# Four transfers of 8 to 15 small packets, issued by ScalarE in the middle of a rotary-embedding kernel

## The chip, the cores and the metric

The kernel runs on one core of one Trainium2 chip. The metric is device time in microseconds (us) of one execution. The core's engines are TensorE (PE; PEld is its weight load), VectorE (DVE), ScalarE (ACT), GpSimd (POOL) and SyncE (SP); 16 transfer (DMA) engines move data between HBM and the on-chip memory. The kernel before ran on the same chip beside the others. Kernels are compared only within the same rounds.

## The reference

Rotary embedding over 16 sequences of 512 rows, 16 heads of 64 values: 32 MiB in, 32 MiB out.

```python
x = x.reshape(batch, seq, num_heads, head_dim)       # 16, 512, 16, 64, float32
x1, x2 = x[..., :half_dim], x[..., half_dim:]
rotated = np.concatenate([x1 * cos - x2 * sin, x1 * sin + x2 * cos], axis=-1)
```

## The kernel before

The work is cut into eight tiles of 4 MiB (128 partitions of 32 KiB, two sequences each). Five buffers hold tiles; a tile is rotated in place and stored from the same buffer. SyncE issues every transfer, in the order written: load 0 in two parts with the two tables between, loads 1 to 4, then stores as tiles become ready. Loads 5 to 7 need buffers whose stores (0 to 2) have landed, so they come behind store 2. The last store is cut in two.

```python
    def load(t, lo=0, hi=KK):
        ...
        nc.sync.dma_start(out=tiles[t][:, s], in_=x_v[t][:, s])

    def store(t, lo=0, hi=KK):
        s = slice(lo * dim, hi * dim)
        nc.sync.dma_start(out=out_v[t][:, s], in_=tiles[t][:, s])
    ...
    def finish(t):
        add(0)
        ...                                  # store(t), the last tile in two parts
        if t + 1 == NT - BUFS:               # behind store 2
            for n in range(BUFS, NT):
                load(n)

    for t in range(NT):                      # NT = 8 tiles
        xt = tiles[t]
        for k in range(KK):                  # 8 rows of 1024 values per partition
            ...   # GpSimd and VectorE multiply by sin, VectorE by cos,
            ...   # TensorE + ScalarE add the two (k = 0 and 4), VectorE adds the rest
            if k == 0 and t > 0:
                finish(t - 1)
            add(1)
    finish(NT - 1)
```

Each transfer raises a completion semaphore when it has landed. The program has eight of them and the tile framework hands them out in turn, to transfers of all issuing engines alike. A transfer that gets a semaphore again waits until the earlier user has landed: in the changed kernel store 3 is next on the semaphore of the first small transfer. The turn goes by the instruction order of the built program, which is not that of the source: the small transfers added below are written behind store 2 and loads 5 to 7, but the built program lists them before store 2.

Of the kernel before, what the change touches and what calls it, by code (L numbers as in the profile page):

```python
# [8 lines left out]
FP32 = mybir.dt.float32  # L9
# [12 lines left out]

FIRST = (3, 8)
LAST_OUT = (4, 8)


@with_exitstack
def kernel(
# [13 lines left out]
    nc = tc.nc  # L42
# [7 lines left out]
    NT = batch // NB  # L50
# [5 lines left out]
    sin_v = sin.rearrange("(p k) j -> p (k j)", k=KK)  # L56

    fixed = ctx.enter_context(tc.tile_pool(name="fixed", bufs=1))
# [10 lines left out]
    def load(t, lo=0, hi=KK):  # L69
        if tiles[t] is None:  # L70
            tiles[t] = xp.tile([P, F], FP32, name="xt")
# [6 lines that stand above are left out]
# [15 lines left out]
    for i in range(3):  # L93
        ps = pe.tile([P, BANK], FP32, name="ps")
        nc.tensor.matmul(out=ps, lhsT=zero[:, :P], rhs=zero, start=True, stop=True)  # L95

    sns = fixed.tile([P, KK, 2, half], FP32)
    tab = pfix.tile([P, BANK], FP32)
    cos_t = tab[:, : KK * half]
# [14 lines left out]
    def cos_b(k, n):  # L114
        c = cos_t[:, k * half : (k + 1) * half]
        return bass.AP(tensor=c.tensor, offset=c.offset, ap=[c.ap[0], [0, n], [1, half]])

    def over_heads(s):
        return bass.AP(tensor=s.tensor, offset=s.offset, ap=[s.ap[0], [0, nh], [1, hd]])

    def swapped(r, n):
        return bass.AP(
            tensor=r.tensor, offset=r.offset + half, ap=[r.ap[0], [hd, n], [-half, 2], [1, half]]
        )

    def swapped_signed(k):

        i = on_dve.index(k)
        s = sns_t[:, i * hd : (i + 1) * hd]
        return bass.AP(  # L130
            tensor=s.tensor, offset=s.offset + half, ap=[s.ap[0], [0, nh], [-half, 2], [1, half]]
        )

    def pairs(r):
        return r.rearrange("p (a j) -> p a j", j=half)

    def halves(r):
        return r.rearrange("p (h a j) -> p h a j", a=2, j=half)
# [3 lines left out]
    def add(most):  # L142
        while len(pending) > most:
            r, ps, b = pending.pop(0)
            nc.vector.tensor_tensor(out=r, in0=ps, in1=b, op=ALU.add)  # L145

    def finish(t):
        add(0)
        lo = 0
        for hi in LAST_OUT if t == NT - 1 else (KK,):  # L150
            store(t, lo, hi)
            lo = hi
        if t + 1 == NT - BUFS:
            for n in range(BUFS, NT):
                load(n)

    for t in range(NT):
        xt = tiles[t]
        for k in range(KK):
            r = xt[:, k * dim : (k + 1) * dim]  # L160
            own = k in DVE_B[t % 2]
            if not own:
                b = bp.tile([P, dim], FP32, name="b")
                sk = sns[:, k].rearrange("p a j -> p (a j)")
                nc.gpsimd.tensor_tensor(out=halves(b), in0=swapped(r, nh), in1=over_heads(sk), op=ALU.mult)  # L165
            if k in PE_ROWS[t % 2]:
                parts = []
                for c in range(0, dim, BANK):
                    ps = pe.tile([P, BANK], FP32, name="ps")
                    rc = r[:, c : c + BANK]  # L170
                    nc.vector.tensor_tensor(  # L171
                        out=pairs(ps), in0=pairs(rc), in1=cos_b(k, BANK // half), op=ALU.mult
                    )
                    parts.append((ps, rc, swapped(rc, BANK // hd) if own else b[:, c : c + BANK]))
                if own:
                    nc.vector.tensor_tensor(out=halves(r), in0=halves(r), in1=swapped_signed(k), op=ALU.mult)  # L176
                for ps, rc, rhs in parts:
                    nc.tensor.matmul(out=ps, lhsT=ident, rhs=rhs, start=False, stop=True, skip_group_check=True)  # L178
                    nc.scalar.copy(out=rc, in_=ps)  # L179
            else:  # L180
                add(1)
                ps = pd.tile([P, dim], FP32, name="pd")
                nc.vector.tensor_tensor(out=pairs(ps), in0=pairs(r), in1=cos_b(k, 2 * nh), op=ALU.mult)  # L183
                pending.append((r, ps, b))
            if k == 0 and t > 0:
                finish(t - 1)
            add(1)
    finish(NT - 1)


# [33 lines left out]
```

## Time and profile before

| | kernel before |
|---|---|
| time, first three runs | 162.77 us median (162.58 to 162.78) |
| span in the profile | 160.8 us |
| transfers | 20, moving 67.26 MB in 2754 packets |
| rate | 418 GB/s over the span, 434 GB/s between landings |
| transfer engines busy | 97.9% of the span |
| VectorE / GpSimd / ScalarE busy | 88% / 81% / 12% |

The prediction below shows the lines and how to read them.

### The profile page before, as it was taken

The page shows a single profiled execution, that of the slowest core. Times are in us where ns is not written, and L with a number is a line of the kernel's source. Part 1 is how long each engine was busy: PE and PEld are TensorE (multiplying, and loading weights), DVE is VectorE, ACT ScalarE, POOL GpSimd, SP SyncE. Part 2 cuts the span into 40 slices and gives each one's busy share as a digit, 9 for nine tenths or more (in the row PEclk, how much of TensorE's full clock was granted, in tenths as well). Part 3 has the DMA queues.
Part 4 walks back from the last instruction along what each step waited for, and adds up shares of the span by engine and source line. Part 5 has one row for each costly group of instructions (what it writes and reads, how often), then busy time and mean ns, then how long its engine had stood idle before and what let it go on. Part 6 is the DMA issues. An engine that isn't in the chain of part 4 may idle for free. (4 is left out here: it accounts for less than half of the span.)

```text
span 160.8 us, 524 instructions
## 1 busy us (share of the span) xinstructions
PE 62.3 (39%) x71; PEld 20.0 (12%) x71; DVE 141.4 (88%) x142; ACT 20.0 (12%) x33; POOL 130.3 (81%) x62
## 2 busy tenths in 40 slices
PE   3045380546217260708035440918053721735000
PEld 0022020202011110202020200211020201111000
DVE  1059999999999999999999999999999999999800
ACT  0110220021102020111102020112002110202000
POOL 1039999999999999999999899999999799950000
PEclk9999958576956755595555555555955585587655
DMA  5999999999999999999999999999999999999994
GB/s 186 395 423 463 408 481 416 391 497 416 391 489 416 402 416 481 408 391 505 399 399 481 424 399 475 424 408 432 465 399 432 465 408 432 457 416 408 428 428 179
DMA packets 2754, 67.26 MB, mean 418 GB/s; under 512 B 320, under 2 KB 448, under 8 KB 448
## 3 DMA queue, kind: packets, MB, share of 16 engines
q1 hardware_dynamic: 2752, 67.24, 97.9%
q14 instruction: 2, 0.02, 0.0%
HBM read 33.69 MB, written 33.55 MB: 418 GB/s over the span
## 5 line engine op out<-in xcount | busy, mean ns | idle before, releaser
L165 POOL TENSOR_TENSOR b<-xt,sns 128x1024 f32<-128x1024 f32 x56 | 129.6, 2358 | 11.8 <-DVE sns L108 9.4
L183 DVE TENSOR_TENSOR pd<-xt,tab 128x1024 f32<-128x1024 f32 x48 | 58.1, 1225 | 0.8
L145 DVE TENSOR_TENSOR xt<-pd,b 128x1024 f32<-128x1024 f32 x48 | 58.4, 1218 | 0.0
L178 PE MATMUL ps<-xt,ident 128*128 128x512 f32 x32 | 29.5, 1077 | 48.6 <-issue 38.1
L178 PE MATMUL ps<-b,ident 128*128 128x512 f32 x32 | 29.4, 1073 | 29.8 <-DVE ps L171 27.1
L179 ACT COPY xt<-ps 128x512 f32<-128x512 f32 x32 | 18.7, 585 | 120.3 <-PE ps L178 120.3
L171 DVE TENSOR_TENSOR ps<-xt,tab 128x512 f32<-128x512 f32 x32 | 20.6, 688 | 0.0
L178 PEld LDWEIGHTS ps<-xt,ident 128*128 128x128 f32 x32 | 9.4, 324 | 68.2 <-issue 63.6
L178 PEld LDWEIGHTS ps<-b,ident 128*128 128x128 f32 x32 | 9.2, 316 | 49.7 <-issue 25.6
L176 DVE TENSOR_TENSOR xt<-xt,tab 128x1024 f32<-128x1024 f32 x8 | 9.8, 1221 | 0.4
L107 DVE TENSOR_SCALAR sns<-tab 128x256 f32<-128x256 f32 x1 | 0.4, 424 | 8.2 <-PE tab L105 8.2
L104 PE MATMUL tab<-b,spread 64*128 64x256 f32 x2 | 1.2, 696 | 5.1 <-DMA b<-in_sin_dram 5.1
L179 ACT ACT_TABLE_LOAD x1 | 1.3, 1283 | 7.3 <-DMA xt<-in_x_dram 7.3
L95 PE MATMUL ps<-zero 128*128 128x512 bf16 x3 | 1.5, 626 | 1.2 <-DVE zero L92 1.2
L104 PEld LDWEIGHTS tab<-b,spread 64*128 64x128 f32 x2 | 0.5, 307 | 6.0 <-issue 6.0
L105 PE MATMUL tab<-b,spread 64*128 64x256 f32 x2 | 1.1, 631 | 0.0
L92 DVE MEMSET zero<- 128x256 uint32 x1 | 0.3, 272 | 0.9 <-PEq L205 0.9
L105 PEld LDWEIGHTS tab<-b,spread 64*128 64x128 f32 x2 | 0.7, 333 | 0.2
L103 DVE COPY spread<-ident 64x64 f32<-64x64 f32 x2 | 0.3, 184 | 0.2 <-POOL ident masks.py:199 0.2
L95 PEld LDWEIGHTS <-zero 128*128 128x128 bf16 x3 | 0.3, 124 | 1.5 <-DVE zero L92 1.2
masks.py:197 POOL MEMSET ident<- 128x128 f32 x1 | 0.2, 205 | 0.3 <-POOLq L205 0.3
L108 DVE COPY sns<-tab 128x256 f32<-128x256 f32 x1 | 0.4, 414 | 0.0
(6 smaller groups left out, 0.9 us busy)
## 6 DMA issues: line engine op xcount, KB each, us to landing
xt<-in_x_dram SPq DMA_DIRECT2D x7, 4096.0 KB, 29.1
out_dram<-xt SPq DMA_DIRECT2D x7, 4096.0 KB, 23.6
out_dram<-xt SPq DMA_DIRECT2D x2, 2048.0 KB, 8.1
xt<-in_x_dram SPq DMA_DIRECT2D x1, 2560.0 KB, 11.5
xt<-in_x_dram SPq DMA_DIRECT2D x1, 1536.0 KB, 6.5
b<-in_sin_dram SPq DMA_DIRECT2D x1, 64.0 KB, 6.5
b<-in_cos_dram SPq DMA_DIRECT2D x1, 64.0 KB, 6.3
```

The costliest lines, as they stand in the source:

```text
L95: nc.tensor.matmul(out=ps, lhsT=zero[:, :P], rhs=zero, start=True, stop=True)
L104: nc.tensor.matmul(out=sin_t, lhsT=spread, rhs=sin_sb, start=True, stop=True)
L105: nc.tensor.matmul(out=cos_t, lhsT=spread, rhs=cos_sb, start=True, stop=True)
L107: nc.vector.tensor_scalar_mul(out=sns[:, :, 0, :], in0=sin_k, scalar1=-1.0)
L108: nc.vector.tensor_copy(out=sns[:, :, 1, :], in_=sin_k)
L145: nc.vector.tensor_tensor(out=r, in0=ps, in1=b, op=ALU.add)
L165: nc.gpsimd.tensor_tensor(out=halves(b), in0=swapped(r, nh), in1=over_heads(sk), op=ALU.mult)
L171: nc.vector.tensor_tensor(out=pairs(ps), in0=pairs(rc), in1=cos_b(k, BANK // half), op=ALU.mult)
L176: nc.vector.tensor_tensor(out=halves(r), in0=halves(r), in1=swapped_signed(k), op=ALU.mult)
L178: nc.tensor.matmul(out=ps, lhsT=ident, rhs=rhs, start=False, stop=True, skip_group_check=True)
L179: nc.scalar.copy(out=rc, in_=ps)
L183: nc.vector.tensor_tensor(out=pairs(ps), in0=pairs(r), in1=cos_b(k, 2 * nh), op=ALU.mult)
```

## The change

Four transfers of 15, 14, 12 and 8 rows of 64 bytes, from the sin table in HBM into a tile that nobody reads, issued by ScalarE behind its work on tile 3. They put small packets on a second queue amid large ones, and bring the program to 24 transfers. The result is not affected.

```diff
+SMALL = (15, 14, 12, 8)
 ...
+    spare = fixed.tile([16, len(SMALL), 16], FP32)
     sns = fixed.tile([P, KK, 2, half], FP32)
 ...
             add(1)
+        if t == NT // 2 - 1:
+            for i, n in enumerate(SMALL):
+                nc.scalar.dma_start(out=spare[:n, i], in_=sin_v[:n, :16])
     finish(NT - 1)
```

## The prediction

The sum below is 162.77 us plus 0.2 us, 163.0 us. The 0.2 us is the estimate, 4 x (46 + 9) ns from packet durations in the trace of before; that one engine gets one packet of each small transfer was an assumption, as the records don't name the engine. The other of "both cases" under *Waits* was a landing some 3 us after the issue, an estimate that the trace of before does not show. A "ring", there and below, is the queue that one issuing engine fills: q1 on the page is SyncE's, and q10 on the page of the changed kernel is ScalarE's.

> **What bounds the kernel now.** I began with the page, because its second part shows at once which resource is never idle. VectorE (DVE) and the transfers both look full in the middle, so the page alone does not decide between them:
>
> ```profile
> span 160.8 us, 524 instructions
> PE 62.3 (39%) x71; PEld 20.0 (12%) x71; DVE 141.4 (88%) x142; ACT 20.0 (12%) x33; POOL 130.3 (81%) x62
> DVE  1059999999999999999999999999999999999800
> DMA  5999999999999999999999999999999999999994
> DMA packets 2754, 67.26 MB, mean 418 GB/s; under 512 B 320, under 2 KB 448, under 8 KB 448
> q1 hardware_dynamic: 2752, 67.24, 97.9%
> ```
>
> The DVE row runs out two slices (8 us) before the end; the DMA row holds to the last slice. One queue, fed by SyncE, keeps 16 transfer engines busy 97.9% of the span. ScalarE (ACT), which gets the new work, is busy 12%.
>
> Next I read the windows view over the end, to see what the span waits for there (columns: window, its length, busy us of PE, PEld, DVE, ACT, POOL with counts, TensorE clock, DMA share, GB/s):
>
> ```profile
> 137.00:147.00 10.00, 6.18 (x8) 1.71 (x6) 9.93 (x10) 1.76 (x3) 5.50 (x3) 0.68 0.99 429
> 147.00:152.00 5.00, 0.03 (x1) 0.00 (x0) 4.97 (x5) 0.59 (x1) 0.00 (x0) 0.81 0.93 400
> 152.00:158.50 6.50, 0.00 (x0) 0.00 (x0) 0.07 (x1) 0.00 (x0) 0.00 (x0) 0.50 0.98 421
> 158.50:160.80 2.30, 0.00 (x0) 0.00 (x0) 0.00 (x0) 0.00 (x0) 0.00 (x0) 0.50 0.02 7
> ```
>
> After 152 us only transfers are left, and they move data at nearly full rate until 158.5. Whether these bytes were a backlog or the natural length of the last store is told by the transfer view, asked for narrow windows so that it answers for one issue at a time, with the timeline of SyncE's queue for the moments of issue. Two of these pairs, the store of tile 3 and the second half of the last store (timeline: start, length; transfer view: KB, us from issue to landing):
>
> ```profile
> 83.97 0.34 SPq L77 DMA_DIRECT2D out_dram<-xt  x1
> out_dram<-xt SPq DMA_DIRECT2D x1, 4096.0 KB, 37.0
> ...
> 152.14 0.33 SPq L77 DMA_DIRECT2D out_dram<-xt  x1
> out_dram<-xt SPq DMA_DIRECT2D x1, 2048.0 KB, 7.6
> ```
>
> Adding issue and landing for every late transfer gives landings at 91.9 (load 5), 101.6 (load 6), 111.3 (load 7), 121.0, 130.6, 140.3, 150.0 (stores 3 to 6), 154.8 and 159.7 us (the halves of store 7). They come in the order of issue, 9.7 us apart per 4 MiB and 4.9 per 2 MiB, that is 434 GB/s, with no gap. So the transfers form one full queue from 67 us to the end, and the last half, issued at 152.1, had to wait until the half before it was through at about 154.8. **The bound is the transfer engines' throughput**; VectorE would have to be later by at least the better part of a microsecond before it showed. Conversely each 0.1 us that the transfer engines lose after that point should move the end by about 0.1 us.
>
> [...]
>
> **The change, part by part.** Nothing is removed. Four transfers are added to ScalarE's instruction order, behind its last copy for tile 3, and one small tile (256 bytes a partition) that nobody reads.
>
> *Issue on ScalarE.* The neighbouring ScalarE rows in the timeline of before:
>
> ```profile
> 76.61 0.58 ACT L179 COPY xt<-ps 128x512 f32<-128x512 f32 x1 [1.12 <-PE ps L178]
> 84.95 0.59 ACT L179 COPY xt<-ps 128x512 f32<-128x512 f32 x1 [7.75 <-PE ps L178]
> ```
>
> The gap runs from 77.19 to 84.95 us, 7.75 us. SyncE's issues took 0.33 to 0.89 us each; four make 1.3 to 3.6 us. They fit, so no copy is delayed: 0 us on the path.
>
> *Bytes.* 15+14+12+8 = 49 packets of 64 bytes, 3.1 KB against 67.2 MB: nothing. What counts is packets per engine. In the trace's records of single packets, a 1 KB packet took 46 ns (median of 128), a 4-byte completion write 9 ns, and a 32 KB packet 1213 ns. Taking the 1 KB duration as a generous size for 64 bytes, an engine that takes part in all four gets 4 x (46 + 9) = 220 ns. Since an even share of the big transfers lies on every engine, the engine with the most extra work sets the end: **+0.2 us**, estimated from these durations. [...]
>
> *Waits.* Completion semaphores are handed out in turn from eight. I compared the instruction order with its waits. The added transfers take four of them, so later transfers sit on others. New waits on the path of SyncE: store 2 now waits on the semaphore of load 3 (before: of the cos table), load 5 also on that of load 4. Loads 3 and 4 were issued near 4 us and landed 39.0 and 48.2 us later (the transfer view gives 48.2 as the longest of all loads, and medians of pairs for the rest), so by 43 and 53 us, while store 2 is issued at 66.4: no cost. Store 3 must wait for the first small transfer, store 4 for the second, stores 5 and 6 for the third and fourth. Only store 3 is close: the small one is issued near 77.2 and the store at 83.97, a margin of 6.8 us. [...] And were it stuck behind the whole backlog, to about 102 us (landing of load 6), store 3 would be issued late but load 7 would still keep the engines full to 111 us: 0 us at the end in both cases.
>
> *Outside the span.* The run takes 162.55 us against a span of 160.8. Another issuing engine might add a little setup or clearing there; I found no number for it and allow a few tenths in the range only.
>
> Sum: 162.77 + 0.2 = **163.0 us**.
>
> **The rivals.** (a) *Wholly hidden*: [...] For it: tens of nanoseconds against 1213 ns packets. It would give 162.7 to 162.8, barely distinguishable. (b) *Changing ring drains the engine*: if an engine must finish outstanding work before it serves the other ring, each small packet could cost a good part of a 1.2 us packet. [...] For it: nothing before used two rings, so it is not excluded. Against: consecutive packets of one ring, loads beside stores, run without gaps, so deep draining is not the engine's habit. (c) *A shared completion holds SyncE up*: store 3 waits for a small transfer that lands late. As worked out this costs nothing unless the delay passes 111 us. (d) *ScalarE holds up PSUM*: were issuing to block ScalarE beyond 84.95 us, TensorE, then VectorE would wait for a free buffer; at most about a microsecond of that is hidden in the backlog at the end. (e) *Faster*: transfers are already at 434 GB/s and 97.9% busy. A gain over 2% (3.3 us) has no place to come from.
>
> **Range and chances.** The low end, 162.4, is rival (a) less a little under the spread of the three runs of before (162.58 to 162.78). The high end, 164.4, lets each of four small packets cost 0.4 us rather than 0.055 on the fullest engine, or a few tenths of setup and a partial ring change together. Beyond 2%, 166.0, a small packet would have to cost 0.8 us on the busiest engine, that is rival (b) at two thirds strength, or (d): 5%. Faster by over 2%: 1%. Within 2%: 94%.
>
> **What would show each step.** Right: about 49 more data packets under 512 bytes, plus completions, on a second queue whose share is near zero; four issues on ScalarE inside its gap after tile 3, with its next copy still near 84.95; store 3 issued near 84 on VectorE's release; landings still 9.7 us apart, with one step near the small transfers 0.2 us longer. Wrong: a step between landings longer by a microsecond or more around 77 to 90 us (rival b); SyncE waiting for a small transfer after 84 us (c); ScalarE idle released by its own queue, and later VectorE gaps (d). The prediction fails if [...] the rate between landings falls after the small transfers; I know no reason for it in this trace.

## The result, and the profile after

| | before | after |
|---|---|---|
| median of 6 runs | 162.68 us (162.51 to 162.92) | 162.42 us (162.32 to 162.80) |
| ratio after / before | | 0.9987, 95% interval 0.9973 to 1.0001 |
| span in the profile | 160.8 us | 160.7 us |

A ratio is the mean time of one kernel's fast runs over the mean of the other's fast runs of the same rounds, so it is not quite the ratio of the medians quoted beside it. The page of the changed kernel, in the lines that answer to those shown of before:

```profile
span 160.7 us, 531 instructions
PE 62.1 (39%) x71; PEld 20.0 (12%) x71; DVE 141.4 (88%) x142; ACT 20.0 (12%) x33; POOL 130.3 (81%) x62
DMA  5999999999999999999999999999999999999994
DMA packets 2852, 67.26 MB, mean 419 GB/s; under 512 B 418, under 2 KB 546, under 8 KB 546
q1 hardware_dynamic: 2752, 67.24, 97.9%
q10 hardware_dynamic: 98, 0.00, 0.0%
```

A second queue, q10, has appeared. It carries 98 packets: 49 of 64 bytes and 49 completion writes. Those 98 are exactly the growth of the count under 512 bytes (320 to 418). No engine's busy time moved by more than 0.2 us, and the main queue is at the same 97.9%.

The timeline of ScalarE and its queue around the four transfers (start and length in us; the bracket is the idle time before), and below it the transfer view of the first small one and the timeline and transfer view of store 3, as before asked in narrow windows:

```profile
76.45 0.58 ACT L182 COPY xt<-ps 128x512 f32<-128x512 f32 x1 [1.12 <-PE ps L181]
76.46 2.92 ACTq L193 DMA_DIRECT2D spare<-in_sin_dram  x4
84.79 0.58 ACT L182 COPY xt<-ps 128x512 f32<-128x512 f32 x1 [7.75 <-PE ps L181]
```

```profile
spare<-in_sin_dram ACTq DMA_DIRECT2D x1, 0.9 KB, 5.7
...
83.80 0.34 SPq L79 DMA_DIRECT2D out_dram<-xt  x1
out_dram<-xt SPq DMA_DIRECT2D x1, 4096.0 KB, 37.2
```

The issues took 2.9 us and fit in ScalarE's gap, which has kept its length of 7.75 us and its releaser, TensorE. (The first was issued while the copy before it still ran.) The first small transfer landed 5.7 us after its issue, at 82.2 us, and store 3 was issued at 83.80 us: 1.6 us were left. Store 3 lands 37.2 us later, at 121.0 us, as before. There is no added wait.

The trace's records of single packets give a finer measure than the time of a run. Take the 32 KB packets in the order of their starts, 16 at a time (there are 16 transfer engines), and call 16 of them a round, placed at their mean start. From store 2's first round to store 6's last it is 76.41 us before and 76.42 us after. Two more traces without small transfers, those of runs 1 and 3 below, have 76.32 and 76.49 us. So the four small transfers cost less than 0.1 us in this stretch, which holds all of them.

### The profile page after: what moved, and what is told of

Read it like the earlier page. It is cut to its first block, busy times and chain, and to the rows that moved or that the text cites. A ratio compares the mean times of both kernels' runs of the same rounds, so it can differ in the third digit from the quotient of the medians.

```text
span 160.7 us, 531 instructions
## 1 busy us (share of the span) xinstructions
PE 62.1 (39%) x71; PEld 20.0 (12%) x71; DVE 141.4 (88%) x142; ACT 20.0 (12%) x33; POOL 130.3 (81%) x62
## 3 DMA queue, kind: packets, MB, share of 16 engines
q1 hardware_dynamic: 2752, 67.24, 97.9%
```

## The experiments

**Theory H**: the transfer engines set the end, and the small packets cost about what their records last. In these records each 64-byte packet took 11 ns and each completion write 9 ns, so an engine that serves one packet of each of the four transfers spends 4 x 20 ns = 0.08 us (an estimate). **Rivals**: the 0.22 us of the prediction (46 ns a packet); a real gain, from layout or from elsewhere (F); a cost of the second ring or of transfers with fewer packets than the 16 engines; and, as the thing that could make such transfers dear at all, **theory S**: small transfers take places in the rotation of eight semaphores and make large ones wait.

### 1. How small a difference can be seen: the kernel before against itself

No edit.

> The unchanged kernel before, as its own opponent, to learn how small a difference five rounds can show. Any theory expects a ratio of 1.000. If the ratio's interval excludes 1.000 or its centre is off by 0.001 (0.16 us), the measured -0.13% of the change is of the size of this error and nothing is to be read into its sign.

Measured: 162.46 us (162.38 to 162.58), ratio 0.9993 (0.9981 to 1.0006). The kernel before had 162.52 us (162.36 to 162.90, 9 runs). So identical kernels differ by 0.0007, with an interval of 0.0012 to either side: 0.2 us is about the limit of what five rounds can tell.

### 2. The changed kernel again

One blank line added.

> The changed kernel once more (one blank line added). Theory H (the small packets are hidden or cost what their records last, 4 x 20 ns = 0.08 us on the fullest engine): ratio 0.9995 to 1.0010. The prediction's sum (+0.22 us): ratio 1.0014. Rival F (the change really makes it faster by a quarter of a microsecond, by whatever cause): 0.9985 again.

Measured: 162.35 us (162.31 to 162.43), ratio 0.9986 (0.9972 to 0.9999). The +0.14% of the prediction's sum is outside the interval a second time. A saving cannot be read from this with confidence: against the twin of the kernel before the medians differ by 0.11 us and the ranges overlap.

### 3. The spare tile alone

```diff
-        if t == NT // 2 - 1:
-            for i, n in enumerate(SMALL):
-                nc.scalar.dma_start(out=spare[:n, i], in_=sin_v[:n, :16])
```

> Only the spare tile, which moves the other tiles of its pool by 256 bytes a partition; no transfers. If the layout is what moved the time by -0.13%, this shows -0.13% as well; if the difference was error, ratio 1.000 within 0.001.

Measured: 162.52 us (162.34 to 162.53), ratio 0.9994 (0.9982 to 1.0007). No effect of the layout is seen. If the 0.1 to 0.2 us by which the changed kernel came out lower is real, it comes from somewhere else; no run here settles that.

### 4. Sixteen rows in each small transfer

```diff
-SMALL = (15, 14, 12, 8)
+SMALL = (16, 16, 16, 16)
```

> The four transfers with 16 rows each[...]. Theory H: as the changed kernel, 162.4 to 162.8 us, 64 data packets and 64 completions on ScalarE's queue. If partial use of the engines (15, 14, 12, 8) mattered, this differs from the changed kernel of the same call by more than 0.3 us.

Measured: 162.30 us (162.24 to 162.41), ratio 0.9983 (0.9971 to 0.9996). It is within 0.05 us of the changed kernel of the same call. The trace records 64 data packets and 64 completions on q10; which engines served them, the records read here don't tell. That a transfer has 15, 14, 12 or 8 rows rather than 16 is not what matters.

### 5. The same four, issued by SyncE

```diff
-                nc.scalar.dma_start(out=spare[:n, i], in_=sin_v[:n, :16])
+                nc.sync.dma_start(out=spare[:n, i], in_=sin_v[:n, :16])
```

> The same four small transfers issued by SyncE, behind load 7, so that there is one ring only. Theory H: they cost nothing visible, 162.4 to 162.8 us; they land in turn behind load 7, near 111 us, and no transfer before store 7 is on their semaphores; store 3 is issued 2 to 3 us later than in the kernel before, at 85 to 87 us, without effect, as the queue is full until 111 us. Rival (changing the ring is what hides or costs something): differs from the changed kernel by more than 0.3 us.

Measured: 162.40 us (162.19 to 162.54) beside 162.54 us, ratio 0.9990 (0.9975 to 1.0005). The timeline of SyncE's queue and the transfer view of the first small one:

```profile
82.72 1.59 SPq L193 DMA_DIRECT2D spare<-in_sin_dram  x4
...
spare<-in_sin_dram SPq DMA_DIRECT2D x1, 0.9 KB, 28.9
```

In SyncE's ring it landed 28.9 us after issue, at 111.6 us, right behind load 7; on ScalarE's own ring it had landed after 5.7 us. So SyncE's ring was served in order here, and the second ring let the small transfer pass some 29 us of backlog. Time is the same either way.

### 6. The disputed cost by itself, enlarged: 4096 packets of 64 bytes

```diff
-SMALL = (15, 14, 12, 8)
+SMALL = (64, 64, 64, 64)
-    spare = fixed.tile([16, len(SMALL), 16], FP32)
+    spare = fixed.tile([64, len(SMALL), 16, 32], FP32)
-                nc.scalar.dma_start(out=spare[:n, i], in_=sin_v[:n, :16])
+                nc.sync.dma_start(out=spare[:n, i, :, :16],
+                                  in_=sin_v[:n, :].rearrange("p (c j) -> p c j", j=16))
```

> The disputed cost by itself, much enlarged, in SyncE's own ring where no turns are taken: four transfers of 64 rows in 16 pieces of 64 bytes, 256 packets on every engine. If a 64-byte packet costs what its record lasts (11 ns): 256 x 11 = +2.8 us, 165.2 us. If it costs the 46 ns that the prediction took from the 1 KB packets: +11.8 us, 174 us. [...] Store 3 will be issued later than 84 us, which costs nothing before 111 us.

Measured: 165.48 us (165.39 to 165.56) beside 162.54 us: +2.9 us, ratio 1.0179. The records again give 11 ns a packet (median of 4096; 256 an engine if they are spread evenly over the 16). 46 ns, which would have made +11.8 us, is refuted. The sum is not clean, though: issuing so many pieces held SyncE (one issue lasted 17.7 us), and store 3 was issued only at 112.25 us, after load 7 was through:

```profile
82.66 29.50 SPq L193 DMA_DIRECT2D spare<-in_sin_dram  x4
112.25 40.12 SPq L79 DMA_DIRECT2D out_dram<-xt  x6
```

So some of the 2.9 us is an emptied queue, not packets, and 11 ns may be too much rather than too little. The next run was meant to remove that.

### 7. A quarter of the dose

As in 6, with 4 pieces to a row instead of 16: 1024 packets, 64 an engine if they are spread evenly.

```diff
-    spare = fixed.tile([64, len(SMALL), 16, 32], FP32)
+    spare = fixed.tile([64, len(SMALL), 4, 32], FP32)
-                                  in_=sin_v[:n, :].rearrange("p (c j) -> p c j", j=16))
+                                  in_=sin_v[:n, :64].rearrange("p (c j) -> p c j", j=16))
```

> The enlarged dose cut to a quarter, so that SyncE isn't held up while it issues: four transfers of 64 rows in 4 pieces, 64 packets of 64 bytes on every engine, in SyncE's ring. At 11 ns a packet: +0.7 us, 163.2 to 163.3 us. At 46 ns: +2.9 us, 165.5 us. Hidden: 162.5 us. Store 3 should be issued before 90 us, unlike 112 us with the full dose.

Measured: 163.02 us (162.94 to 163.16) beside 162.81 us, ratio 1.0015 (1.0002 to 1.0028), that is +0.24 us with 0.03 to 0.46 possible. SyncE was held for 9.8 us by the small transfers, and then by the issue of store 3 itself (its timeline in a narrow window):

```profile
92.60 15.67 SPq L79 DMA_DIRECT2D out_dram<-xt  x1
```

That issue began at 92.60 us, where under 90 was expected, and ended only at 108.27 us. This is still before load 7 was through, near 111 us, and the rounds of packets show no emptied queue: from load 7's last round to store 3's first it took 1.72 us, where the kernel before has 1.25 us; with the full dose of (6) it took 4.69 us. The 46 ns (+2.9 us) are refuted here without the confusion. The 0.7 us of 64 x 11 ns are not quite reached: in the time +0.24 us; in the rounds, from store 2's first to store 6's last, 76.96 us against 76.32 to 76.49 us without small transfers, that is 0.5 to 0.6 us or 7 to 10 ns a packet. How much of a packet's time is hidden stays open at this precision. For four packets on an engine, both say: below a tenth of a microsecond.

### 8. Sixteen pieces to a row: how two rings share an engine, and what waiting on a small transfer costs

```diff
-    spare = fixed.tile([16, len(SMALL), 16], FP32)
+    spare = fixed.tile([16, len(SMALL), 16, 32], FP32)
-                nc.scalar.dma_start(out=spare[:n, i], in_=sin_v[:n, :16])
+                nc.scalar.dma_start(out=spare[:n, i, :, :16],
+                                    in_=sin_v[:n, :].rearrange("p (c j) -> p c j", j=16))
```

> Each row of a small transfer in 16 pieces of 64 bytes: 16 packets instead of 1 on each engine that takes part. Theory T (an engine gives ScalarE's ring one small packet per 32 KB packet of SyncE's ring, 1.2 us): each transfer needs 17 turns, about 21 us; the first lands near 101 us and store 3 is issued then, store 4 near 121, store 5 near 132 (when SyncE's ring runs dry, the rest goes at once), store 6 near 143 instead of 137; SyncE is seen waiting for small transfers, and the run takes 165 to 169 us. Rival P (pieces of one row go together in one turn): the first lands near 83 us, nothing waits, 162.4 to 162.9 us.

Measured: 162.97 us (162.90 to 163.34) beside 162.54 us, ratio 1.0031 (1.0016 to 1.0046). The waits of SyncE (us in total, times, longest us), the transfer view of the first small one, and SyncE's queue at stores 3 to 6:

```profile
SPq L79 <- DMA spare<-in_sin_dram: 38.2, 3, 19.0
...
spare<-in_sin_dram ACTq DMA_DIRECT2D x1, 15.0 KB, 25.3
...
101.55 0.34 SPq L79 DMA_DIRECT2D out_dram<-xt  x1
...
119.88 0.34 SPq L79 DMA_DIRECT2D out_dram<-xt  x1
121.67 0.33 SPq L79 DMA_DIRECT2D out_dram<-xt  x1
136.56 0.33 SPq L79 DMA_DIRECT2D out_dram<-xt  x1
```

The turns are as theory T said. The first small transfer, issued at 76.2 us, landed after 25.3 us, at 101.5 us, and store 3 was issued at 101.55 us where the changed kernel has 83.80 us. Fifteen more pieces to a row took 25.3 - 5.7 = 19.6 us longer, 1.3 us each: about one 32 KB packet (1.21 us) per small one. Rival P, one turn for all pieces, would have landed near 83 us.

Theory T's time was wrong. Store 4 came at 119.88 us as expected (121), but stores 5 and 6 were expected near 132 and 143 us and came at 121.67 and 136.56 us. SyncE's ring ran dry already around 120 us, when store 3 was nearly through and store 4 had only just been issued; in that moment the remaining small packets went through at once (of the 833 packets of q10, 355 lie in 116 to 121 us and 9 behind that), and the later stores were held no more. Two stores issued 18 us late and one 2.5 us late, with the small packets, cost 0.43 us (0.26 to 0.75 by the ratio). So a late issue cost little as long as the queue had other work. The packets have their part in this: while the queue was still full, from store 2's first round to load 7's last, it took 37.89 us, where the ten other traces (all but that of (9)) have 37.57 to 37.68 us. That is 0.2 to 0.3 us for some 25 small packets and completion writes on an engine (an estimate, from turns of 1.3 us), 8 to 13 ns each. Taking turns between two rings thus cost nothing visible beyond the packets' own 11 ns.

### 9. Eight small transfers

```diff
-SMALL = (15, 14, 12, 8)
+SMALL = (15, 14, 12, 8, 15, 14, 12, 8)
```

> Twice the list, eight small transfers, 28 in all. Theory H alone (a small packet costs next to nothing): at most +0.2 us, 162.4 to 162.9. Theory S (what small transfers can cost is a place in the rotation of eight completion semaphores): the instruction order shows store 2 now on the semaphore of the first small transfer, so store 2, ready at 66.3 us, waits until that has landed, near 79 us, and loads 5 to 7 queue up behind it. Store 1 lands at 72.4 us and leaves the transfer engines idle for some 7 us, load 5 lands near 99 us instead of 91.9, and the run takes 168 to 171 us.

Measured: **172.07 us** (171.89 to 172.32) beside 162.54 us, ratio 1.0587 (1.0571 to 1.0603). The waits of SyncE and GpSimd, SyncE's queue, and the windows view between store 1's landing and the restart (columns as in the prediction; the last two are DMA share and GB/s):

```profile
SPq L79 <- DMA spare<-in_sin_dram: 28.8, 1, 28.8
...
POOL b L168 <- DMA xt<-in_x_dram: 8.4, 1, 8.4
...
77.75 0.33 SPq L79 DMA_DIRECT2D out_dram<-xt  x1
78.27 12.05 SPq L75 DMA_DIRECT2D xt<-in_x_dram  x3
...
66.00:72.00 6.00, 2.72 (x4) 0.62 (x2) 5.97 (x6) 1.17 (x2) 6.00 (x3) 0.75 0.81 350
72.00:73.00 1.00, 0.47 (x1) 0.50 (x2) 1.00 (x3) 0.00 (x0) 1.00 (x2) 0.68 0.00 0
...
77.00:78.00 1.00, 0.00 (x0) 0.00 (x0) 0.97 (x2) 0.00 (x0) 1.00 (x2) 1.00 0.03 2
82.00:90.00 8.00, 3.66 (x4) 1.17 (x4) 7.97 (x9) 1.17 (x2) 8.00 (x5) 0.71 1.03 394
```

Here is why, in the listing of SyncE's instructions with their waits (DMAHW are the eight completion semaphores), for the changed kernel and for this one:

```
changed kernel, store 2:  DMACopy out_0_dram<-xt_84 128x8192 [waits DMAHW5_49,DMAHW6_49,DVE_49,Activation_49]
eight small,    store 2:  DMACopy out_0_dram<-xt_84 128x8192 [waits DMAHW2_49,DMAHW5_49,DVE_49,Activation_49]
both, first small:        DMACopy spare_103<-in_sin_dram 15x16 [waits DMAHW2_49]
```

In the changed kernel store 2 follows load 3 on semaphore 6, and load 3 landed long ago. With eight small transfers the rotation has gone once round, and store 2 follows the *first small transfer* on semaphore 2. ScalarE issues that one at 76.1 us, behind its work on tile 3. (The listing is made by building the two kernels; in it the small transfers stand before store 2.) So store 2, ready near 66 us, was issued at 77.75 us, and loads 5 to 7 stood behind it. The transfer engines ran out of work: a share of 0.81 instead of 1.01 over 66 to 72 us, which is 1.2 us, and next to none from 72 to 78 us, 6 us more. (The wait of 28.8 us is counted from SyncE's issue before, store 1; all but some 11 us of it is the wait that store 2 has anyway.) Load 5 came late, and GpSimd waited 8.4 us for it where the kernel before had it wait 0.4 us.

The expected range of 168 to 171 us was too low by 1 us. The span grew by 9.0 us (169.7 against 160.7), and idle engines explain 7.2 us of it. After the restart some packets also took longer: 1.03 of a share moved only 394 GB/s in 82 to 90 us, and the main queue was busy for 93.7% of 169.7 us = 159.0 us against 97.9% of 160.7 us = 157.3 us, which is 1.7 us more. The packet records place nearly all of it in four rounds: at 87.2 and 89.2 us, where store 2 gives way to load 5, the mean packet took 1.95 and 1.34 us instead of 1.21, and at 116.0 and 117.5 us, where load 7 gives way to store 3, 1.46 and 1.79 us. After the restart the 16 packets of a round start within about 0.1 us of each other. Whether that is why these changes between loads and stores cost more than in the kernel before was not tested.

### 10. Eight again, without that wait

```diff
-        if t == NT // 2 - 1:
+        if t in (NT // 2 - 1, 5):
...
-                nc.scalar.dma_start(out=spare[:n, i], in_=sin_v[:n, :16])
+                nc.scalar.dma_start(out=spare[:n, i + (0 if t < NT // 2 else len(SMALL))], in_=sin_v[:n, :16])
```

(with a spare tile for eight)

> Eight small transfers as in the run that took 172.07 us, but four behind tile 3 and four behind tile 5. The instruction order shows that the second four follow the first on the same semaphores and that store 2 keeps the wait it has in the changed kernel (load 3). Theory S (the 9.5 us came from store 2 waiting for a small transfer): 162.3 to 162.9 us, store 2 issued at 66.2 us and no idle stretch of the transfer engines near 72 to 78 us. Rival N (eight small transfers on ScalarE's ring are in themselves expensive): 166 us or more.

Measured: 163.05 us (162.96 to 164.05) beside 162.81 us (162.52 to 163.04), ratio 1.0035 (1.0005 to 1.0065), in which one run of 164.05 weighs; the other three are 162.96 to 163.09. The upper end of the expectation is passed by 0.15 us on a chip whose kernel before was 0.1 to 0.3 us slower than in the other calls. Store 2 is back at 66.35 us:

```profile
66.35 0.33 SPq L79 DMA_DIRECT2D out_dram<-xt  x1
66.84 15.92 SPq L75 DMA_DIRECT2D xt<-in_x_dram  x3
```

The same eight small transfers cost 9.5 us or a few tenths, depending on which later transfer comes behind them in the rotation. (The second four also stand later in time; the idle stretch of (9) and its wait point to the rotation.) Theory S holds and rival N falls.

## Why the prediction was right, point by point

- **The bound.** Right. Holding stores back by 18 us cost 0.43 us (8), while in (9) the queue was empty for 7.2 us and its packets took 1.7 us longer, and the span grew by 9.0 us: what the transfer engines lose moves the end by as much.
- **The estimate of +0.2 us** is the term that was mis-sized. It took 46 ns for a 64-byte packet from the 1 KB packets, "as a generous size". Records show 11 ns, so 0.08 us for four of them with their completion writes of 9 ns, and (7) and (8) measure 7 to 13 ns a packet. The measured ratio has its interval's upper end at 1.0001, below the predicted 1.0014. The time, 162.42 us, is only 0.02 us above the low end of the range: rival (a), "wholly hidden", describes it best. That the time fell inside the range is partly luck, because the kernel before alone moves by more than this from call to call.
- **Issue on ScalarE.** Right: 2.92 us, inside the predicted 1.3 to 3.6 us, in a gap of 7.75 us.
- **The waits.** Right that store 2 and load 5 pay nothing and that store 3 is the close one. The landing some 3 us after the issue (the estimate, with one 1.2 us packet to wait for) was too hopeful: it took 5.7 us, and of a margin that came out as 7.3 us only 1.6 us was left. In the packet records the first small packet starts 4.0 us after the issue, the length of more than three large packets, and the last of its fifteen completion writes comes 5.2 us after it; in (9), with the engines idle, the first packet starts after 1.0 us. Why the first turn comes so late is open. The further claim, that a late store 3 would cost nothing before 111 us, fits the store issued at 101.55 us in (8), though the 0.43 us of that run aren't fully taken apart.
- **Rivals (b), (c), (d).** (b), a ring change that drains the engine, is refuted: a turn for a small packet costs 8 to 13 ns (8), not a good part of 1.2 us, and issue through one ring or two takes the same time (ratio 0.9990 in (5), 0.9987 for the changed kernel). (c) is real as a mechanism but not in this change; (8) and (9) produce it on purpose, with store 3 issued 18 us and store 2 11 us late. (d) did not occur: ScalarE's idle time before its next copy is 7.75 us as before.
- **Outside the span.** Nothing was seen: time minus span is 1.7 us with the second queue (162.43 - 160.7) and 1.75 us without (162.55 - 160.8), the same within the rounding of the spans.
- **What it missed.** It weighed the semaphores only for the four transfers as given. It did not see that four more in the same place would turn a harmless change into one of +5.9%.

## What to carry to other kernels

In this kernel a few tiny transfers beside a full queue of large ones cost nothing that could be measured (ratios 0.9987 and 0.9990), whether ScalarE or SyncE issued them. What they can cost, 9.5 us in (9), is a place in the rotation of completion semaphores: build the program, list which earlier transfer each later one has to follow, in the built order, and look for a large, early one that now follows a small, late one. A transfer issued late cost little here as long as the queue did not run empty: 0.43 us in (8), for 18 us.
